# The attention branch's gate by 1024 columns, with block products on seven of sixteen k-tile pairs

## The chip, the cores and the metric

The kernel runs on one core of one Trainium2 chip. The metric is device time in microseconds (us), the median of several executions. Lower is better.

## The reference

One block of a hybrid transformer, in float32, for 256 tokens of width 2048 with a context of 256 tokens. The block normalises and modulates its input (an adaptive layer norm whose shift, scale and gate vectors come from `silu(c) @ w_ada`), projects it with `w_in`, runs a bidirectional gated recurrence (8 heads) and a windowed attention (8 heads) beside one another, merges the two branches, and ends in a convolutional feed-forward part. What matters here is the merge:

```
def gated_merge(y_rec, y_att, gate_rec, gate_att, w_rec, w_att, w_o):
    y = jax.nn.sigmoid(gate_rec) * (y_rec @ w_rec) + jax.nn.sigmoid(gate_att) * (y_att @ w_att)
    return y @ w_o
```

`gate_att` is a slice of the input projection: the modulated input (256 x 2048) times a 2048 x 2048 matrix. `y_rec @ w_rec` and `y_att @ w_att` contract over 1024.

## The kernel before

**Numbers as two halves.** TensorE multiplies rounded float32. Every operand is held as a high part (`hi`, a rounded copy) and a low part (`lo`, the rest), and `mm3` (L72) makes one product of three matmuls: high by high, high by low, low by high. A weight block arrives as 128 x 1024 float32 values in a buffer `raw` (five of them); ScalarE copies it to `whi` and VectorE subtracts to get `wlo` (three buffers each). Below, "a product" is such a three-matmul `mm3` on one 128 x 128 tile of activations and 512 columns of weights.

**The order of the work.** The program is written as one long Python trace. A scheduler orders the instructions of each engine at build time by priority (the place in the trace) and readiness; at run time every engine takes its list strictly in order. `tc.high_priority(offset=n)` moves instructions forward by n places; weight loads are moved by `LEAD` = 60, modulation steps by `LAG` = 60 the other way, a few evacuations by `RUSH` = 120. `issue_after` keeps an order on one engine.

**Weights.** `Stream.load` (L110) fetches the next 1024 columns of the weight stream on SP's queue and splits them. `chunk` (L141) does the same for parts that need something else in front of the split: it calls `make(raw)`, then casts and subtracts, each after the chunk before it (`behind`). Both read the same stream `wst`, whose order is laid down by the host code (L1207 to L1245).

**Modulation steps.** The vectors of the later modulations (gate 1, scale 2, shift 2, gate 2) are not made by TensorE matmuls but one block at a time: `ada_steps` (L387) is a generator with 8 groups of 19 steps. Sixteen steps of a group each load 512 KB of `w_ada` through POOL's DMA queue into a buffer `araw` and add it, times one column of `silu(c)`, to `acc` on VectorE (L405, L407). Two steps do nothing, and the last one transposes `acc` with TensorE and reduces it (L415 to L422). `ada(n)` takes n steps; it is called in many places, and `Stream.load` calls it too, once for every 16 points, where each load adds `st.pace` points. `homes[0]` says how many buffers the steps may use: 4 (two `araw` buffers and the tiles tagged `kT` and `va`) or 2 (the `araw` buffers alone). Groups 0 to 3 must be done when the merged result is added to x, groups 4 and 5 at its tile 10, the rest when the down projection begins.

**Small tasks.** Work such as transposing a result or the inner steps of a recurrent head is put in the list `tasks`; `tick` runs one at fixed points of the big matmul loops, for instance once per pass of `natural` (L466).

**The stages around the change.** The recurrent heads h = 0 to 7 (L691 to L722): for each, two loops `tform_all` of 48 matmuls, with `hgrn_a` (ScalarE and VectorE) behind each and `hgrn_b` to `hgrn_e` as tasks; after each `hgrn_a`, `ada(1)` for heads 0, 6 and 7 and `ada(2)` for heads 1 to 5 (L713), then `ada(1)` per head. Then attention, the recurrent output's gate, and the recurrent branch's merge gate (L820), four times 512 columns. Then the merge loop over four groups of 512 columns (L838 to L853): for each c, `columns()` makes the attention branch's gate (16 k-tiles, two blocks of 128 tokens, 96 matmuls) and applies a sigmoid; `columns(head(yre), 8)` makes the recurrent product (48 matmuls) and `columns(head(yat), 8)` the attention product (48); VectorE multiplies and adds (L845, L847, L848). All through this loop `st.pace` is 8, so every second load takes a modulation step. After it `xm` (x itself, 2 MB) is loaded into the tile tagged `qo`, which until then holds the recurrent output.

**The block product that exists already.** The first 32 of the 44 k-tiles of the feed-forward's down projection are done by `down_two` and `half` (L968, L1032). Two k-tiles and the two token blocks form a 2 x 2 block of activations, and two k-tiles and two groups of 512 columns a 2 x 2 block of weights. A normal pair takes 8 products. For the seven pairs in `SEVEN` a scheme with seven products is used: the activations are summed beforehand (`seven_acts`, L948), the weights on the fly by VectorE (`four`, L1010: four additions of 128 x 512, into two `araw` buffers), so three `chunk` splits beside the half one stand in place of two. Four banks `norm` and four banks `sev` collect the products, and eight VectorE additions and one copy (L1023 to L1030) join them.

**PSUM.** Eight banks: five in pool `mm` (`bankm`) and three in pool `ms` (`banks`).

Of the kernel before, what the change touches and what calls it, by code (L numbers as in the profile page):

```python
# [7 lines left out]
F32 = mybir.dt.float32  # L8
# [6 lines left out]
P = 128  # L15
# [20 lines left out]
SEVEN = (1, 3, 5, 7, 9, 11, 13)  # L36

# [14 lines left out]
def block_kernel(ctx, tc, xct, prm, cst, ada2, wst, out):  # L52
# [105 lines left out]
    def split(hi, lo, src):  # L158
        S.copy(hi, src)
        V.tensor_tensor(lo, src, hi.bitcast(F32), op=ALU.subtract)  # L160

# [529 lines left out]
    for h in range(H):  # L691
# [14 lines left out]
        for d in range(2):  # L706
            if 2 * h + d < 3:
                o = early_f[2 * h + d]
            else:
                o = bank()  # L710
                tform_all(o)
            hgrn_a(h, d, o)
            ada(1 if h > 5 or not h else 2)  # L713
# [104 lines left out]

    grn = gr.rearrange("p (c a b) t -> p c a (b t)", c=4, a=2)
    for c in range(4):  # L820
# [8 lines left out]
        if c == 2:  # L829
# [25 lines left out]
    st.pace = 0  # L855
    with tc.issue_after(sig.ins):
# [111 lines left out]
    def half(g0, g1, norm, sev, y, own):  # L968
# [4 lines left out]

        def add(b, a, w, start=False, stop=False):
            mm3(b, *a, *w, start, stop)
        first = SEVEN[0]
        for p in range(16):
            k1, k2 = 2 * p, 2 * p + 1
            rb, (w21, w22) = chunk(2, fetch)
            a11, a21, a12, a22 = act(k1, 0), act(k1, 1), act(k2, 0), act(k2, 1)  # L980
            if p not in SEVEN:
                st0, sp = p == 0, p == 15
                if sp:
                    ra, (w11, w12) = chunk(2, fetch)
                    for b, u1, u2, v1, v2 in ((0, a11, a12, w11, w21), (1, a11, a12, w12, w22), (2, a21, a22, w11, w21),
                                              (3, a21, a22, w12, w22)):
                        add(norm[b], u1, v1)
                        add(norm[b], u2, v2, stop=True)
                    break
                add(norm[0], a12, w21, st0)  # L990
                add(norm[2], a22, w21, st0)
                add(norm[1], a12, w22, st0)
                add(norm[3], a22, w22, st0)
                ra, (w11, w12) = chunk(2, fetch)
                add(norm[0], a11, w11)
                add(norm[2], a21, w11)
                add(norm[1], a11, w12)
                add(norm[3], a21, w12)
                continue
            f, l = p == first, p == SEVEN[-1]  # L1000
            d = sums[p]
            s1, s2, s4 = [(d[:, 0, i * P:i * P + P], d[:, 1, i * P:i * P + P]) for i in range(3)]
            add(norm[0], a12, w21)
            add(norm[1], s4, w22)
            ra, (w11,) = chunk(1, fetch, home=own)
            add(sev[0], a11, w11, f, l)

            r4 = strm.tile([P, 1024], F32, name="araw", bufs=2)

            def four(raw):  # L1010
# [249 lines left out]
```

## Time and profile before

| | |
|---|---|
| Median of 3 runs | 1665.86 us (1665.86 to 1666.29) |
| Profiled execution | 1666.65 us, of which its span is 1664.9 us |
| Granted TensorE clock | 1.00 |
| Matmuls | 8981, PE busy 99% of the span |
| VectorE (DVE) busy | 75% |
| ScalarE (ACT) busy | 50% |
| DMA | 372.83 MB, mean 224 GB/s |
| Merge loop, three of its four groups | 683.0 to 819.6 us |

PE stands for TensorE's matmuls and PEld for its weight loads, which run beside them. A group of instructions is named by line, engine, operation and `out<-in` with the program's tile names; behind the bar stand busy time, the mean duration of one in ns, and the time that the engine stood idle just before them, with what ended that wait. Rows of stretches (A:B) give busy time and, in brackets, instructions of each engine, then the granted clock, the DMA engines' share and GB/s. Matmuls are pipelined and overlap in the record, so their pitch is read from start times and not from durations. Nearly all matmuls come from the helper on L70, and all split copies and subtractions from L115, L116, L149 and L150; they are told apart by tile names.

### The profile page before, as it was taken

The numbers are of one execution on the slowest core, as the hardware profiler recorded it, in microseconds if no ns is written. First come the engines' busy times: TensorE is split into PE (matmuls) and PEld (weight loads), VectorE is DVE, ScalarE is ACT, GpSimd is POOL, SyncE is SP. The second block draws the span as 40 slices with busy tenths as digits, with TensorE's granted clock in tenths as the row PEclk, the third lists the DMA queues.
The fourth block names the chain that finished last, engine by engine and source line by source line (L and its number), as shares of the span: only waits on it lengthen the run. The fifth ranks groups of instructions, "written<-read, shape, count | busy, mean of one in ns | idle before, by whom it ended". The sixth has DMA issues, their size and how long they took to land.

```text
span 1664.9 us, 23855 instructions
## 1 busy us (share of the span) xinstructions
PE 1648.2 (99%) x8981; PEld 1369.6 (82%) x8981; DVE 1241.8 (75%) x1914; ACT 838.2 (50%) x1267; POOL 68.1 (4%) x132
## 2 busy tenths in 40 slices
PE   8999999999999999999999999999999999999998
PEld 4668888888888888888888988888888888888887
DVE  3448986666879876768769887788776888986655
ACT  4336543444645654444445665555555555545542
POOL 0000100000000000001100000000000000000000
PEclk9999999999999999999999999999999999999999
DMA  9996834534466666977856567577555665655554
GB/s 379 407 372 233 301 114 156 189 114 152 165 214 210 223 213 227 335 238 277 286 203 232 186 216 266 200 278 263 192 180 187 202 214 197 222 196 190 187 189 148
DMA packets 104723, 372.83 MB, mean 224 GB/s; under 512 B 11536, under 2 KB 13728, under 8 KB 104608
## 3 DMA queue, kind: packets, MB, share of 16 engines
q1 hardware_dynamic: 86176, 304.20, 51.8%
q0 software_dynamic: 18432, 67.12, 12.4%
q8 instruction: 70, 1.15, 0.3%
q14 instruction: 45, 0.37, 0.1%
HBM read 369.16 MB, written 2.11 MB: 223 GB/s over the span
## 4 chain that ended last, share of the span: by engine, by line
PE 89%; DVE 4%; issue 3%; DMA 2%; ACT 1%; POOL 0%; SPq 0%; DVEq 0%; ACTq 0%; POOLq 0%
PE bankm L70 78%; PE banks L70 9%; DVE wlo L116 1%; DMA ringv<-in_wst_dram 1%; DMA ringkT<-in_wst_dram 1%; DVE acc L407 1%; PE banks L782 0%; PE banks L415 0%; DMA araw<-in_ada_dram 0%; DMA ringq<-in_wst_dram 0%; PE banks L615 0%; PE banks L810 0%; PE banks L607 0%; DMA xraw<-in_xct_dram 0%; PE banks L1080 0%
## 5 line engine op out<-in xcount | busy, mean ns | idle before, releaser
L116 DVE TENSOR_TENSOR wlo<-raw,whi 128x1024 fp32r<-128x1024 f32 (+2 forms) x410 | 499.0, 1218 | 228.7 <-ACT whi L115 225.5
L115 ACT CAST whi<-raw 128x1024 fp32r<-128x1024 f32 (+2 forms) x410 | 428.3, 1045 | 459.0 <-PE bankm L70 411.7
L70 PE MATMUL bankm<-hl,whi 128*128 128x512 f32 (+1 forms) x2048 | 627.7, 389 | 0.1
L70 PE MATMUL bankm<-whi,hl 128*128 128x512 f32 x1640 | 526.4, 393 | 1.0 <-ACT hl L252 0.9
L70 PE MATMUL bankm<-hl,wlo 128*128 128x256 f32 (+2 forms) x1760 | 396.6, 293 | 1.5 <-DVE wlo L116 1.5
L70 PEld LDWEIGHTS bankm<-hl,wlo 128*128 128x128 f32 x1760 | 330.8, 188 | 75.6 <-DVE wlo L116 2.4
L70 PEld LDWEIGHTS bankm<-whi,hl 128*128 128x128 f32 x1640 | 307.4, 188 | 66.1 <-ACT hl L252 2.6
L70 PEld LDWEIGHTS bankm<-hl,whi 128*128 128x128 f32 x2048 | 327.8, 189 | 17.8 <-DVE fs L916 0.4
L70 PE MATMUL bankm<-wlo,hl 128*128 128x512 f32 x820 | 320.3, 391 | 0.0
L70 PEld LDWEIGHTS bankm<-wlo,hl 128*128 128x128 f32 x820 | 154.1, 188 | 31.2 <-DVE wlo L116 0.2
L407 DVE SCALAR_TENSOR_TENSOR acc<-araw,csil,acc 128x1024 f32<-128x1024 f32 x120 | 153.5, 1279 | 2.1 <-DMA araw<-in_ada_dram 1.7
L150 DVE TENSOR_TENSOR wlo<-raw,whi 128x1024 fp32r<-128x1024 f32 x74 | 90.2, 1224 | 41.2 <-ACT whi L149 38.9
L402 POOL DMA_DIRECT2D araw<-in_ada_dram x128 | 67.9, 531 | 1091.4 <-DVE acc L407 569.3
L149 ACT CAST whi<-raw 128x1024 fp32r<-128x1024 f32 x74 | 77.7, 1053 | 66.4 <-PE bankm L70 41.1
L70 PE MATMUL bankm<-yb,whi 128*128 128x512 f32 x256 | 80.9, 397 | 0.0
L70 PEld LDWEIGHTS bankm<-yb,wlo 128*128 128x128 f32 x256 | 48.1, 188 | 11.2
L929 ACT ACTIVATE fs<-fs,prm 128x256 f32<-128x256 f32 x44 | 26.4, 601 | 52.0 <-DVE fs L464 52.0
L70 PE MATMUL bankm<-yb,wlo 128*128 128x256 f32 x256 | 50.6, 279 | 0.0
L149 ACT CAST whi<-araw 128x1024 fp32r<-128x1024 f32 x28 | 29.4, 1052 | 39.0 <-DVE araw L1012 34.9
L70 PE MATMUL banks<-whi,hl 128*128 128x512 f32 x136 | 46.3, 389 | 0.0
L70 PE MATMUL bankm<-whi,g 128*128 128x512 f32 x124 | 41.3, 390 | 0.0
L70 PEld LDWEIGHTS bankm<-yb,whi 128*128 128x128 f32 x256 | 39.2, 189 | 0.1
(291 smaller groups left out, 1523.3 us busy)
## 6 DMA issues: line engine op xcount, KB each, us to landing
raw<-in_wst_dram SPq DMA_DIRECT2D x489, 512.0 KB, 4.1
araw<-in_ada_dram POOLq DMA_DIRECT2D x128, 512.0 KB, 4.7
ringv<-in_wst_dram SPq DMA_DIRECT2D x24, 512.0 KB, 10.0
ringq<-in_wst_dram SPq DMA_DIRECT2D x20, 512.0 KB, 9.9
araw<-in_wst_dram SPq DMA_DIRECT2D x10, 512.0 KB, 9.9
xraw<-in_xct_dram SPq DMA_DIRECT2D x8, 512.0 KB, 6.9
raw<-in_wst_dram SPq DMA_DIRECT2D x7, 384.0 KB, 9.9
ringkT<-in_wst_dram SPq DMA_DIRECT2D x5, 512.0 KB, 9.9
```

The lines of the kernel that those rows point to most:

```text
L70: return PE.matmul(o, l, r, start=start, stop=stop, skip_group_check=True)
L115: S.copy(hi, raw)
L116: self.last = V.tensor_tensor(lo, raw, hi.bitcast(F32), op=ALU.subtract)
L149: a = S.copy(hi[:, w], raw[:, w])
L150: b = V.tensor_tensor(lo[:, w], raw[:, w], hi[:, w].bitcast(F32), op=ALU.subtract)
L402: nc.gpsimd.dma_start(raw, ada2[idx])
L407: V.scalar_tensor_tensor(acc, raw, csil[:, kt, 0:1], acc, op0=ALU.mult, op1=ALU.add)
L929: S.activation(t, s, AF.Identity, bias=cb[:, f:f + 1], scale=cw[:, f, 1:2])
```

## The change

`half` is taken out of the end of the kernel and made general: it gets the function that picks activations, the number of pairs, the list of pairs done by seven products, their sums, the banks, the destination and the buffer for a lone half chunk. The down projection uses it as before. The merge loop now uses it for the attention branch's gate: for c = 0 and c = 2 it makes 1024 columns at once (8 pairs of k-tiles, two token blocks, four destination tiles `y`), with pairs 2, 4 and 6 by seven products for c = 0 and pairs 0, 2, 4 and 6 for c = 2. The sigmoids of all four tiles follow; c = 1 and c = 3 find theirs ready.

The sums of the activations are made once for both by four new tasks, `gate_sums`, which run in the last group of the recurrent branch's merge gate. They lie in a tile tagged `qo`, which `xm` takes afterwards. The half chunk's buffer takes the tag `kT`, so the modulation steps have two buffers (`homes[0] = 2`) through the merge loop.

Since `chunk` does not add to the pace, the 16 modulation steps that fell into the gates' columns are no longer taken there: `ada(2)` becomes `ada(3)` in heads 1 to 5, which is ten steps, and the other six fall to the calls behind the merge loop. The host lays the gate's weights out in the order in which the pairs read them.

```
+GSEVEN = (2, 4, 6), (0, 2, 4, 6)
...
+    def half(act, n, seven, sums, banks, y, own):
+        norm, sev = banks
...
+        for p in range(n):
+            k1, k2 = 2 * p, 2 * p + 1
+            rb, (w21, w22) = chunk(2, fetch)
+            a11, a21, a12, a22 = act(k1, 0), act(k1, 1), act(k2, 0), act(k2, 1)
+            st0 = p == 0
+            if p not in seven:
...
+            f, l = p == seven[0], p == seven[-1]
+            if f:
+                sev = sev()
+            s1, s2, s4, *s3 = sums[p]
+            add(norm[0], a12, w21, st0)
+            add(norm[1], s4, w22, st0)
+            ra, (w11,) = chunk(1, fetch, home=own)
+            add(sev[0], a11, w11, f, l)
+            r4 = strm.tile([P, 1024], F32, name="araw", bufs=2)
+            def four(raw):
+                V.tensor_tensor(raw[:, 0:512], ra[:, 0:512], ra[:, 512:], op=ALU.add)
+                V.tensor_tensor(raw[:, 512:], ra[:, 512:], rb[:, 512:], op=ALU.add)
+                V.tensor_tensor(r4[:, 0:512], raw[:, 0:512], rb[:, 512:], op=ALU.add)
+                V.tensor_tensor(r4[:, 512:], r4[:, 0:512], rb[:, 0:512], op=ALU.add)
+            r2, (t1, t3) = chunk(2, four, "araw")
+            add(sev[1], s1, t1, f, l)
+            add(sev[3], s3[0] if s3 else a21, t3, f, l)
+            _, (t2, t4) = chunk(2, lambda raw: None, r4)
+            add(sev[2], s2, t2, f, l)
+            add(norm[2], a22, t4, st0)
...
-            ada(1 if h > 5 or not h else 2)
+            ada(1 if h > 5 or not h else 3)
...
+    def gate_sums(p):
+        if not gsums:
+            gsums["all"] = big.tile([P, 4, 2, 4 * P], F32R, name="sx", tag="qo")
+        d = gsums["all"][:, len(gsums) - 1]
+        x = scr.tile([P, 512], F32, name="t")
+        w = scr.tile([P, 512], F32, name="t")
+        V.tensor_tensor(x.rearrange("p (k t) -> p k t", k=2), hl[:, 2 * p:2 * p + 2, 1, :].bitcast(F32),
+                        hl[:, 2 * p:2 * p + 2, 0, :].bitcast(F32), op=ALU.add)
+        a11, a21, a12, a22 = [x[:, i * P:i * P + P] for i in range(4)]
+        V.tensor_tensor(w[:, 0:P], a21, a22, op=ALU.subtract)
+        V.tensor_tensor(w[:, P:2 * P], a11, w[:, 0:P], op=ALU.subtract)
+        V.tensor_tensor(w[:, 2 * P:3 * P], a12, w[:, P:2 * P], op=ALU.subtract)
+        V.tensor_tensor(w[:, 3 * P:], a21, a11, op=ALU.subtract)
+        split(d[:, 0, :], d[:, 1, :], w)
+        gsums[p] = parts_of(d[:, 0], d[:, 1])
...
+            tasks += [lambda p=p: gate_sums(p) for p in (2, 4, 6, 0)]
...
+    homes[0] = 2
+    gown = big.tile([P, 2, 512], F32R, name="gone", tag="kT")
+    gown = [gown[:, i] for i in range(2)]
     for c in range(4):
-        gas = []
-        for o in columns():
-            ga = scr.tile([P, 512], F32, name="t")
-            sig = S.activation(ga, o, AF.Sigmoid)
-            gas.append(ga)
+        if c % 2 == 0:
+            norm = [bank() for _ in range(4)]
+            y = [scr.tile([P, 512], F32, name="t") for _ in range(3)] + [scr.tile([P, 512], F32, name="rs", bufs=1)]
+            half(tok, 8, GSEVEN[c // 2], gsums, (norm, lambda: [bank()] + [bank(ms) for _ in range(3)]), y, gown)
+            for o in y:
+                sig = S.activation(o, o, AF.Sigmoid)
         for tt, o in enumerate(columns(head(yre), 8)):
             V.tensor_tensor(grn[:, c, tt, :], grn[:, c, tt, :], o, op=ALU.mult)
         for tt, o in enumerate(columns(head(yat), 8)):
-            V.tensor_tensor(gas[tt], gas[tt], o, op=ALU.mult)
-            V.tensor_tensor(grn[:, c, tt, :], grn[:, c, tt, :], gas[tt], op=ALU.add)
+            ga = y[2 * tt + c % 2]
+            V.tensor_tensor(ga, ga, o, op=ALU.mult)
+            V.tensor_tensor(grn[:, c, tt, :], grn[:, c, tt, :], ga, op=ALU.add)
...
+    homes[0] = 4
     with tc.issue_after(sig.ins):
         S.preload_act_table_set("natural_log_exp_and_others")
...
+    gat = ga_a.reshape(8, 2, P, 2, 1024)[:, ::-1].transpose(3, 0, 1, 2, 4).reshape(2, 16, P, 1024)
     for c in range(4):
-        parts += [gat[c], wr[c], wt[c]]
+        parts += ([gat[c // 2]] if c % 2 == 0 else []) + [wr[c], wt[c]]
```

More of the change, by code (lines that the diff above doesn't have):

```diff
@@ L162, in exp_silu, with parts_of @@
+    def parts_of(hi, lo):
+        return [(hi[:, i:i + P], lo[:, i:i + P]) for i in range(0, hi.shape[-1], P)]
     def exp_silu(dst, src, tmp):
@@ L817, in turned @@
             V.scalar_tensor_tensor(lo, o2, scale, hi.bitcast(F32), op0=ALU.mult, op1=ALU.subtract)
+    gsums = {}
+    def gate_sums(p):
[13 more added lines that the diff above has]
+        gsums[p] = parts_of(d[:, 0], d[:, 1])
     grn = gr.rearrange("p (c a b) t -> p c a (b t)", c=4, a=2)
@@ L966, in up, with down_two @@
             up_evac(g, gt, i, *duo((h2, h2)))
-    def half(g0, g1, norm, sev, y, own):
+    def down_two(g0, g1):
+        own = big.tile([P, 2, 512], F32R, name="wone", tag="acc")
+        own = [own[:, i] for i in range(2)]
         def act(k, tt):
@@ L972, in act @@
             return gt[:, k % 16, 1, ts], gt[:, k % 16, 0, ts]
[L974 to L1010, printed above, removed]
-                V.tensor_tensor(raw[:, 0:512], ra[:, 0:512], ra[:, 512:], op=ALU.add)
-                V.tensor_tensor(raw[:, 512:], ra[:, 512:], rb[:, 512:], op=ALU.add)
-                V.tensor_tensor(r4[:, 0:512], raw[:, 0:512], rb[:, 512:], op=ALU.add)
-                V.tensor_tensor(r4[:, 512:], r4[:, 0:512], rb[:, 0:512], op=ALU.add)
-            r2, (t1, t3) = chunk(2, four, "araw")
-            add(sev[1], s1, t1, f, l)
-            add(sev[3], a21, t3, f, l)
-            _, (t2, t4) = chunk(2, lambda raw: None, r4)
-            add(sev[2], s2, t2, f, l)
-            add(norm[2], a22, t4)
-            if l:
-                S.copy(y[0], sev[0])
-                V.tensor_tensor(y[2], sev[2], y[0], op=ALU.subtract)
-                V.tensor_tensor(y[1], sev[1], y[2], op=ALU.add)
-                V.tensor_tensor(y[2], sev[3], y[2], op=ALU.add)
-                V.tensor_tensor(y[3], sev[3], y[1], op=ALU.add)
@@ L1028, in half @@
-        with tc.high_priority(offset=RUSH):
-            for b in range(4):
-                V.tensor_tensor(y[b], norm[b], y[b], op=ALU.subtract if b == 2 else ALU.add)
-    def down_two(g0, g1):
-        own = big.tile([P, 2, 512], F32R, name="wone", tag="acc")
-        own = [own[:, i] for i in range(2)]
+        both = {p: parts_of(sums[p][:, 0], sums[p][:, 1]) for p in SEVEN}
         sev = [bank()]
@@ L1038, in down_two @@
         y0 = [scr.tile([P, 512], F32, name="t") for _ in range(3)] + [scr.tile([P, 512], F32, name="rs", bufs=1)]
-        half(g0, g1, norm, sev, y0, own)
+        half(act, 16, SEVEN, both, (norm, lambda: sev), y0, own)
         norm = [bank()] + [bank(ms) for _ in range(3)]
@@ L1043, in down_two @@
         y1 = [y1[b // 2][:, b % 2] for b in range(4)]
-        half(g0, g1, norm, sev, y1, own)
+        half(act, 16, SEVEN, both, (norm, lambda: sev), y1, own)
         return y0, y1
@@ L1228 @@
     parts += [aqh[0], aqh[1], flat(_nat(np, gg)), flat(_nat(np, ga_r))]
-    gat, wr, wt = _nat(np, ga_a), _nat(np, g["w_rec_proj"][0]), _nat(np, g["w_att_proj"][0])
+    wr, wt = _nat(np, g["w_rec_proj"][0]), _nat(np, g["w_att_proj"][0])
+    gat = ga_a.reshape(8, 2, P, 2, 1024)[:, ::-1].transpose(3, 0, 1, 2, 4).reshape(2, 16, P, 1024)
     for c in range(4):
-        parts += [gat[c], wr[c], wt[c]]
+        parts += ([gat[c // 2]] if c % 2 == 0 else []) + [wr[c], wt[c]]
     parts.append(_duos(np, _tiles_t(np, g["w_out"][0])))
```

28 lines of the change are left out of this document (added).

## The prediction

> **What bounds the kernel now.** I read the page first (span, busy shares, the chain that ended last, the costliest groups).
>
> ```profile
> span 1664.9 us, 23855 instructions
> PE 1648.2 (99%) x8981; PEld 1369.6 (82%) x8981; DVE 1241.8 (75%) x1914; ACT 838.2 (50%) x1267; POOL 68.1 (4%) x132
> PEclk9999999999999999999999999999999999999999
> PE 89%; DVE 4%; issue 3%; DMA 2%; ACT 1%; POOL 0%; SPq 0%; DVEq 0%; ACTq 0%; POOLq 0%
> ...
> L70 PE MATMUL bankm<-whi,hl 128*128 128x512 f32 x1640 | 526.4, 393 | 1.0 <-ACT hl L252 0.9
> ```
>
> The matmul queue sets the end: 89% of the chain is PE, its clock is granted in full in every slice, and the form that makes the gate (weights `whi` moving, activations `hl` stationary) stood idle 1.0 us in 1640 matmuls. So a matmul taken out is worth its pitch, wherever the queue stays fed. Since busy matmuls overlap, I take the pitch from start times, in the two down-projection halves that already use the block product (timeline, then busy time by stretch: one normal and one seven-product pair each).
>
> ```profile
> 1313.10 0.84 PE L70 MATMUL bankm<-wone,hl 128*128 128x512 f32 x3
> 1313.78 0.39 PE L70 MATMUL banks<-whi,sb 128*128 128x512 f32 x1
> ```
>
> ```profile
> core 0: us, PE busy (x) PEld busy (x) DVE busy (x) ACT busy (x) POOL busy (x), PEclk, DMA share, GB/s
> 1294.95:1305.85 10.90, 10.65 (x47) 7.84 (x45) 9.21 (x13) 7.13 (x11) 0.00 (x0) 1.00 0.58 194
> 1305.85:1316.04 10.19, 10.19 (x46) 8.44 (x45) 9.78 (x13) 5.67 (x8) 0.00 (x0) 1.00 0.62 208
> 1316.04:1326.22 10.18, 10.18 (x46) 8.45 (x45) 9.14 (x10) 5.77 (x7) 0.00 (x0) 1.00 0.63 206
> ```
>
> Three matmuls take 13.78 - 13.10 = 0.68 us, 0.227 each. A normal pair is 24 of them, a seven-product pair 21: 45 x 0.2267 = 10.2 us, which is what a steady stretch takes (edges add one to the count). VectorE is busy 9.14 of 10.18 there and still in time. Only the first stretch, where the block product begins, took 0.72 us longer.
>
> **The change part by part.** *Removed matmuls.* Each of the four 512-column gates was 96 matmuls. Now two gates of 1024 columns take 5 normal and 3 seven-product pairs, then 4 and 4: 183 + 180 = 363 against 384. **21 x 0.2267 = 4.76 us off the path.** The weight bytes and transposes stay the same in number.
>
> The Trainium skill ("TensorE: Matmul & The Clock Gate", Back-to-back issue gap) puts a sustained stream of weight loads and matmuls at about 131 ns a matmul for 512 columns, and calls 216 ns the isolated gap. By 131 ns the saving would be an estimated 2.75 us instead. The timeline above, 227 ns in such a stream, disagrees, and decides.
>
> *VectorE in the two new halves.* Its work per stretch is known from the same stage:
>
> ```profile
> L150 DVE TENSOR_TENSOR wlo<-raw,whi 128x1024 fp32r<-128x1024 f32 x16 | 19.6, 1224 | 3.8 <-ACT whi L149 2.9
> L150 DVE TENSOR_TENSOR wlo<-araw,whi 128x1024 fp32r<-128x1024 f32 x10 | 12.2, 1222 | 0.3
> L150 DVE TENSOR_TENSOR wone<-raw,wone 128x512 fp32r<-128x512 f32 x5 | 3.4, 685 | 0.0
> L1011 DVE TENSOR_TENSOR araw<-raw 128x512 f32<-128x512 f32 x5 | 3.4, 684 | 0.0
> ```
>
> A normal pair is two 1224 ns subtractions; the end of a half adds eight 128x512 operations at 0.685, 5.5 us. First half: 3 x 9.14 + 2 x 2.45 + 5.5 = 37.8 us in 183 x 0.2267 = 41.5. Second: 4 x 9.14 + 5.5 = 42.1 in 40.8. The excess 1.3 us is that end work, which feeds no matmul of the half; it only frees banks, and the ScalarE copy of `sev[0]` frees one first, the early subtraction of `norm[0]` (finished 18 matmuls, 4.1 us, before the half ends) the next. I cost the end at 0, as that cover is longer than an operation; without it, up to 1.4 us each.
>
> *Entering a half.* The first begins with two normal pairs: 10.9 us in which VectorE owes 4.9, so it can catch up by 6.0. The work before it grows by the sums: four times two 128x512 operations and four 128x128 ones.
>
> ```profile
> 639.00:661.00 22.00, 22.00 (x110) 18.11 (x109) 16.84 (x21) 10.14 (x12) 2.12 (x4) 1.00 0.70 241
> 661.00:683.00 22.00, 22.00 (x98) 18.21 (x97) 14.73 (x13) 9.75 (x11) 2.11 (x4) 1.00 1.02 392
> 683.00:728.50 45.50, 45.50 (x206) 37.66 (x205) 34.32 (x33) 19.28 (x21) 4.22 (x8) 1.00 0.82 283
> 728.50:774.00 45.50, 45.50 (x210) 37.63 (x209) 31.37 (x33) 18.89 (x20) 2.64 (x5) 1.00 0.71 244
> ```
>
> ```profile
> L934 DVE TENSOR_TENSOR fs<-fs,fs 128x256 f32<-128x256 f32 x44 | 18.6, 424 | 2.7
> L418 DVE TENSOR_TENSOR modv<-modv,prm 128x8 f32<-128x8 f32 x1 | 0.2, 162 | 0.0
> L407 DVE SCALAR_TENSOR_TENSOR acc<-araw,csil,acc 128x1024 f32<-128x1024 f32 x120 | 153.5, 1279 | 2.1 <-DMA araw<-in_ada_dram 1.7
> ```
>
> A 128x128 operation lies between 0.16 and 0.42; I take the middle, 0.29, so one set is 2 x 0.685 + 4 x 0.29 = 2.5 us and four are 10.1. The last recurrent gate (661 to 683) had 14.73 busy, so 24.8 of 22: 2.8 us over, less than the 6.0 that the two normal pairs give. Price 0, as long as no other 3.2 us comes with it. The lone half chunk's buffer takes `kT`, so it also waits for the last modulation step there; pair 2 comes 10.9 us into the half, and the same 6.0 us cover that step's 1.28.
>
> The second half starts with a seven-product pair at once. Before it, gates 0 and 1 without their own columns hold (34.32 + 31.37) - 16 x 1.224 - 8 x 1.28 = 35.9 us of VectorE in 91.0 - 43.5 = 47.5: not full. Its first block product waits for a PSUM bank that the last attention product of gate 1 still holds: three operations of 0.685 after one 1.22 subtraction at worst, 3.3 us, less the six matmuls (1.4) that go first, 1.9. So entry costs between 0 (a steady stretch) and 0.72 + 1.9 = 2.6; I take **0.72**, the one entry the trace shows.
>
> *Modulation steps.* Blocks fetched by `chunk` do not count for the pace, so 16 steps leave the gate stage: 10 go to heads 1 to 5, 6 further back (up-projection tiles 23 to 27).
>
> ```profile
> araw<-in_ada_dram POOLq DMA_DIRECT2D x128, 512.0 KB, 4.7
> ```
>
> Each step issues one 512 KB DMA on POOL's queue, 4.7 us to landing, and one 1.28 us operation. Heads 1 to 5 get 12.8 us of VectorE and 5.2 MB:
>
> ```profile
> 208.00:241.00 33.00, 32.71 (x284) 27.12 (x283) 26.96 (x71) 17.84 (x37) 1.06 (x2) 1.00 0.27 89
> 241.00:274.00 33.00, 33.00 (x228) 27.91 (x227) 27.69 (x59) 13.01 (x27) 2.64 (x5) 1.00 0.56 189
> 274.00:322.00 48.00, 48.00 (x219) 39.99 (x218) 26.40 (x31) 15.79 (x27) 4.75 (x9) 1.00 0.58 196
> 322.00:366.00 44.00, 44.00 (x336) 36.51 (x335) 33.68 (x83) 21.98 (x43) 1.06 (x2) 1.00 0.26 87
> 433.00:455.00 22.00, 21.47 (x130) 17.74 (x129) 20.68 (x42) 14.50 (x31) 2.64 (x5) 1.00 0.67 227
> ```
>
> From 208 to 366 it was idle 158 - 114.7 = 43.3 us: price 0, and without that cover 12.8 at most. The six that go back leave the sixth group complete only at tile 8 of the merged sum, the last call before its use at tile 10; two tiles of matmuls cover it, else a landing and an operation, 4.7 + 1.28. The tight place is head 7 (433 to 455): PE lost 0.53 to VectorE there.
>
> ```profile
> 454.20 0.33 PE L607 MATMUL banks<-cst,hb 128*128 128x128 f32 x1 [0.53 <-DVE hb L572]
> ```
>
> The shift by 10 puts there steps 55 to 60 of 19-step groups: two empty ones, the transposes and the first of a group in place of six multiply-adds, so less VectorE work. I count 0, with a gain of up to 0.53.
>
> *Queues.* The sums take the buffer that `xm` (two 1 MB loads on SP's queue) needs, so these leave after the second half instead of at 651 us.
>
> ```profile
> L860 SPq DMA_DIRECT2D xm<-in_xct_dram x2: 384/495/606, 651.4 to 654.4; - x2
> 669.06 1.05 ACT L115 CAST whi<-raw 128x1024 fp32r<-128x1024 f32 x1 [2.93 <-DMA raw<-in_wst_dram]
> ```
>
> Weight fetches queue behind them, and ScalarE waited 2.93 us for one; PE was busy all through 661 to 683 all the same, covered by the split tiles ahead. Without that cover it is 2.9 at most. I take 0; `xm` itself has gates 2 and 3, over 40 us.
>
> *Sum.* -4.76 + 0.72 = **-4.04 us**: span 1660.86. The profiled run took 1666.65, so 1.75 lies around its span: 1662.61. The timed median stands 0.79 below that run: **1661.8 us**.
>
> **The rivals.** (B) *The saving in full or more*: entry costs nothing and head 7's 0.53 goes: 1665.86 - 5.29 = 1660.6. For it: 13 VectorE operations stood in the stretch that began late, left over from the up-projection, and these are not here. Against: the second half is entered without a normal pair.
>
> (C) *Given back in small waits*: both entries cost 0.72 and the second also its 1.9 of bank wait: 1665.86 - 4.76 + 3.34 = 1664.4. For it: VectorE is fuller in the second half than in the steady stretches. Against: 34 us of steady alternation without a stall.
>
> (D) *Slower: the two `araw` buffers.* The block product needs both for its summed weights, and modulation steps, no longer allowed the other two homes, use the same two. If steps left over from gate 1 hold them, the second half's first sums wait for a landing and an operation, 4.7 + 1.28 = 6.0 us each; two steps are 12.0. Behind them in the lists of ScalarE and VectorE stand all later splits, since `chunk` keeps their order, and TensorE waits for those. It decides once the delay passes the lead of two split tiles, 24 matmuls or 5.4 us: then 1665.86 - 4.04 + 12.0 - 5.4 = 1668.4. For it: POOL waits on these buffers most of its time.
>
> ```profile
> POOL araw L402 <- DVE acc L407: 569.3, 100, 56.7
> ```
>
> Against: VectorE has over 10 us free in gates 0 and 1 to finish them.
>
> (E) *A removed matmul gives less than its pitch*, because weight loads pace the queue. Then each is worth its busy share in the page, 1369.6/8981 = 0.152 us, 3.2 for the 21, and less the entry 2.5: 1663.4. Against: 45 matmuls in 10.18. The Trainium skill, in the section named above, has the spacing set by weight load and matmul together, which is this case's rule.
>
> **How the numbers follow.** Forecast 45% (own range 1661.1 to 1662.5), B 12%, C 29%, D 12%, E 2%. About 0.2%, 3.3 us, is what a measurement of this kernel can tell from no change. Faster by more is the forecast and B, 57%; within it C and E, 31%; slower D, 12%. Low end: B's 1660.6, less 0.2 for the timing spread of 0.43: 1660.4. High end: through C up to about half of D, 1667.0; this leaves out some 6% above and as much below.
>
> **What would show it.** The profile after should have 8960 matmuls; a steady stretch of 10.2 us in both gate halves; gates 0 to 3 about 4 us shorter from the first sigmoid's stage to the first `xm` operation; PE busy without idle in heads 1 to 5. C shows as gaps where the second half begins, with a wait on a bank or on a `whi` or `wlo`; D as VectorE or ScalarE idle in front of the sums, released by `araw` or its DMA; B as none of these. The forecast is wrong if the stage gains its 4 us and the total does not (then the moved steps cost it in heads 1 to 7), or if PE stands more than 1.4 us in the halves.

## The result and the profile after

The changed kernel takes 1672.02 us (median of 6 runs, 1669.66 to 1672.26), the kernel before in the same series 1665.86 (6 runs, 1664.77 to 1666.29). The ratio is 1.0033, 95% interval 1.0022 to 1.0043: **slower by 6.2 us**, where 4 us less were forecast, and above the range. The profiled execution of the changed kernel is the fastest of its six (1669.66 us), so its trace need not show the whole of the 6.2 us.

From the page of the changed kernel: span, busy time of each engine, and the group of the modulation steps. All later line numbers are this kernel's: products L71, splits L116, L117, L150 and L151, the four weight sums L204 to L207, a step's operation L473.

```profile
span 1667.9 us, 23899 instructions
PE 1648.4 (99%) x8960; PEld 1366.4 (82%) x8960; DVE 1284.4 (77%) x1996; ACT 852.8 (51%) x1287; POOL 68.4 (4%) x132
...
L473 DVE SCALAR_TENSOR_TENSOR acc<-araw,csil,acc 128x1024 f32<-128x1024 f32 x120 | 153.2, 1277 | 1.8 <-DMA araw<-in_ada_dram 1.5
```

The 21 matmuls are gone (8960), the steps are the same 120 with the same duration, and yet the span is 3.0 us longer. TensorE's waits (sum in us, times, longest) have new entries:

```profile
PE banks L71 <- ACT whi L150: 3.8, 2, 3.6
...
PE banks L71 <- DVE hb L635: 0.7, 2, 0.5
PE banks L71 <- DVE hb L621: 0.6, 2, 0.4
...
PE bankm L71 <- ACT whi L116: 0.2, 1, 0.2
```

For comparison, the rows of the same view of the kernel before, whose lines are L70, L116 and L555:

```profile
PE bankm L70 <- DVE wlo L116: 1.5, 2, 0.8
...
PE banks L70 <- DVE hb L555: 0.3, 1, 0.3
```

The wait for `whi` of 3.6 us is new. The ones for `hb`, which belong to the recurrent heads, have grown, and two of them are in new places. The 1.5 us of the kernel before are two waits in the first projections (151 and 161 us), ahead of all that was changed; some of the profiles used here have them and some do not: the kernel before's has them, the changed kernel's has not.

Where the 3.0 us arose can be read from two marks: the last sigmoid of the recurrent branch's gate, and the first operation on `xm` behind the merge loop. Each row gives the first and the last start; the kernel before first, the changed kernel second.

```profile
L828 ACT ACTIVATE gr<-bankm x4: 584/594/600, 636.3 to 663.3; 128x512 f32<-128x512 f32 x4
...
L872 DVE SCALAR_TENSOR_TENSOR xm<-bankm,modv,xm x32: 473/477/485, 852.2 to 932.4; 128x256 f32<-128x256 f32 x32
```

```profile
L912 ACT ACTIVATE gr<-bankm x4: 583/592/600, 638.8 to 665.3; 128x512 f32<-128x512 f32 x4
...
L963 DVE SCALAR_TENSOR_TENSOR xm<-bankm,modv,xm x32: 473/476/486, 855.3 to 935.4; 128x256 f32<-128x256 f32 x32
```

| part of the span | before | after | difference |
|---|---|---|---|
| up to the first mark | 663.3 | 665.3 | +2.0 (+3.5 without the two early waits) |
| between the marks: the changed stage | 188.9 | 190.0 | +1.1 |
| behind the second mark | 812.7 | 812.6 | -0.1 |

The marks are operations of ScalarE and VectorE, and the first comes 0.5 us later behind TensorE's own work in the changed kernel. TensorE's matmuls, counted in the trace, are sharper. The merge loop, from its first matmul to the first one on `yb`, has 768 of them before (662.16 to 840.13 us, 177.97) and 747 after (663.62 to 843.16, 179.54): 1.6 us more. At 170 us, when the two early waits lie behind, the changed kernel is 1.6 us ahead of the kernel before at the same matmul; at the loop's first one it is 1.5 us behind, so 3.1 us are lost between.

So two things went wrong, and apart from one another. The heads, in which nothing was changed but where ten steps stand, lost about 3.1 us. And the stage that has 4.76 us less to do took 1.6 us more, so it lost 6.3 somewhere.

**The place in the stage.** TensorE's timeline where the second half begins (start, duration, operation; in brackets the idle time before it and what ended it):

```profile
754.19 0.40 PE L71 MATMUL banks<-whi,sx 128*128 128x512 f32 x1
758.16 0.80 PE L71 MATMUL banks<-whi,sx 128*128 128x512 f32 x1 [3.57 <-ACT whi L150]
```

It waited 3.57 us for the cast of `t2, t4`, the second pair of weight sums. VectorE's timeline says why these were late:

```profile
745.08 0.68 DVE L482 TENSOR_REDUCE modv<-banks 128x4 f32<-128x512 f32 x1
...
746.46 1.28 DVE L473 SCALAR_TENSOR_TENSOR acc<-araw,csil,acc 128x1024 f32<-128x1024 f32 x1
...
750.00 0.68 DVE L205 TENSOR_TENSOR araw<-raw 128x512 f32<-128x512 f32 x1
...
753.62 0.68 DVE L938 TENSOR_TENSOR gr<-gr,rs 128x512 f32<-128x512 f32 x1
754.22 1.28 DVE L473 SCALAR_TENSOR_TENSOR acc<-araw,csil,acc 128x1024 f32<-128x1024 f32 x1
755.53 0.69 DVE L206 TENSOR_TENSOR araw<-araw,raw 128x512 f32<-128x512 f32 x1
756.26 0.69 DVE L207 TENSOR_TENSOR araw<-araw,raw 128x512 f32<-128x512 f32 x1
```

One group of steps ends here (L482) and the next begins, with the first step (L471) at 745.67 and the second at 746.46. Of the four sums, L204 and L205 run at 749.39 and 750.00; before L206 come five operations for the attention product and the first pair, and then another **step**. POOL's queue shows the load of that step's block:

```profile
746.72 0.53 POOL L468 DMA_DIRECT2D araw<-in_ada_dram  x1 [33.31 <-DVE modv L484]
```

The first two blocks of the new group had lain in the two `araw` buffers since their loads were issued at 710.55 and 712.88, because their steps had to stand behind the old group's transposes and reductions. As soon as the first was read, the third block was loaded into its buffer (the row names L484, which ends 0.1 us behind L471), and it landed 3.8 us later, at 750.5. The program has only these two buffers. L204 and L205 write one of them and L206 still reads it, so L206 and L207 write the other, the one with the step's block, and could not run before the step had read it.

So the second pair of sums is ready at 757, when TensorE has used up all that it had at 754.6. What stands in between is nothing that VectorE waited for: it is busy without a gap. Busy time by stretch (PE, PEld, VectorE, ScalarE, POOL, granted clock, DMA share, GB/s):

```profile
744.50:755.00 10.50, 10.09 (x45) 7.91 (x43) 10.50 (x16) 2.62 (x3) 0.53 (x1) 1.00 0.48 150
755.00:758.20 3.20, 0.04 (x1) 0.04 (x1) 1.95 (x4) 1.14 (x2) 0.00 (x0) 0.99 0.11 19
758.10:761.60 3.50, 3.40 (x7) 2.30 (x8) 3.46 (x3) 1.97 (x4) 0.00 (x0) 0.51 0.45 149
761.60:772.00 10.40, 10.40 (x47) 8.59 (x47) 8.38 (x11) 5.89 (x7) 0.00 (x0) 1.00 0.59 203
```

The third row is the second part of the loss: right behind the stall the granted clock is 0.51, for 3.4 us, and 7 matmuls are started where 15 would be. The page's forty slices do not show it, since each is 42 us long.

### The profile page after: what moved, and what is told of

Read it like the earlier page. It is cut to its first block, busy times and chain, and to the rows that moved or that the text cites. A ratio compares the mean times of both kernels' runs of the same rounds, so it can differ in the third digit from the quotient of the medians.

```text
span 1667.9 us, 23899 instructions
## 1 busy us (share of the span) xinstructions
PE 1648.4 (99%) x8960; PEld 1366.4 (82%) x8960; DVE 1284.4 (77%) x1996; ACT 852.8 (51%) x1287; POOL 68.4 (4%) x132
## 4 chain that ended last, share of the span: by engine, by line
PE 92%; DVE 4%; DMA 2%; issue 1%; ACT 1%; SPq 0%; ACTq 0%; DVEq 0%
PE bankm L71 78%; PE banks L71 11%; DMA ringv<-in_wst_dram 1%; DVE wlo L117 1%; DVE acc L473 1%; DMA ringq<-in_wst_dram 1%; PE banks L848 0%; PE banks L681 0%; PE banks L481 0%; PE banks L673 0%; ACT whi L116 0%; DMA xraw<-in_xct_dram 0%; PE banks L876 0%; PE banks L1112 0%; PE banks L682 0%
## 5 line engine op out<-in xcount | busy, mean ns | idle before, releaser
L71 PE MATMUL bankm<-hl,whi 128*128 128x512 f32 (+1 forms) x2048 | 627.6, 389 | 0.1
L117 DVE TENSOR_TENSOR wlo<-raw,whi 128x1024 fp32r<-128x1024 f32 (+1 forms) x378 | 459.1, 1216 | 184.2 <-ACT whi L116 180.7
L116 ACT CAST whi<-raw 128x1024 fp32r<-128x1024 f32 (+1 forms) x378 | 394.4, 1045 | 397.5 <-PE bankm L71 347.4
L71 PE MATMUL bankm<-whi,hl 128*128 128x512 f32 x1556 | 501.1, 393 | 1.2 <-ACT hl L318 1.0
L71 PE MATMUL bankm<-hl,wlo 128*128 128x256 f32 (+2 forms) x1760 | 396.1, 293 | 0.0
L71 PEld LDWEIGHTS bankm<-hl,wlo 128*128 128x128 f32 x1760 | 330.6, 188 | 73.9 <-DVE wlo L117 0.5
L71 PEld LDWEIGHTS bankm<-whi,hl 128*128 128x128 f32 x1556 | 291.7, 188 | 63.9 <-ACT hl L318 2.6
L71 PEld LDWEIGHTS bankm<-hl,whi 128*128 128x128 f32 x2048 | 327.6, 189 | 17.5 <-DVE fs L1007 0.4
L71 PE MATMUL bankm<-wlo,hl 128*128 128x512 f32 x778 | 303.4, 391 | 0.0
L71 PEld LDWEIGHTS bankm<-wlo,hl 128*128 128x128 f32 x778 | 146.4, 188 | 29.3 <-DVE wlo L117 0.2
L151 DVE TENSOR_TENSOR wlo<-raw,whi 128x1024 fp32r<-128x1024 f32 x99 | 120.7, 1223 | 49.6 <-ACT whi L150 46.3
L473 DVE SCALAR_TENSOR_TENSOR acc<-araw,csil,acc 128x1024 f32<-128x1024 f32 x120 | 153.2, 1277 | 1.8 <-DMA araw<-in_ada_dram 1.5
L150 ACT CAST whi<-raw 128x1024 fp32r<-128x1024 f32 x99 | 104.1, 1054 | 83.3 <-PE bankm L71 51.5
L71 PE MATMUL bankm<-yb,whi 128*128 128x512 f32 x256 | 80.8, 397 | 0.0
L150 ACT CAST whi<-araw 128x1024 fp32r<-128x1024 f32 x42 | 44.1, 1053 | 65.3 <-DVE araw L205 54.3
L71 PEld LDWEIGHTS bankm<-yb,wlo 128*128 128x128 f32 x256 | 48.1, 188 | 11.3
L151 DVE TENSOR_TENSOR wlo<-araw,whi 128x1024 fp32r<-128x1024 f32 x42 | 51.2, 1221 | 2.9 <-ACT whi L150 1.7
L71 PE MATMUL bankm<-yb,wlo 128*128 128x256 f32 x256 | 50.6, 279 | 0.0
L71 PE MATMUL banks<-whi,hl 128*128 128x512 f32 x136 | 46.3, 389 | 0.0
L71 PE MATMUL bankm<-whi,g 128*128 128x512 f32 x124 | 41.3, 389 | 0.0
```

The lines of the kernel that those rows point to most:

```text
L71: return PE.matmul(o, l, r, start=start, stop=stop, skip_group_check=True)
L116: S.copy(hi, raw)
L117: self.last = V.tensor_tensor(lo, raw, hi.bitcast(F32), op=ALU.subtract)
L150: a = S.copy(hi[:, w], raw[:, w])
L151: b = V.tensor_tensor(lo[:, w], raw[:, w], hi[:, w].bitcast(F32), op=ALU.subtract)
L473: V.scalar_tensor_tensor(acc, raw, csil[:, kt, 0:1], acc, op0=ALU.mult, op1=ALU.add)
```

## The experiments

All times are medians, with the ratio to the kernel before on the same chip and its 95% interval. The kernel before took 1666.21 us beside the first four, 1666.04 beside the next three, 1665.58 beside the three after these and 1666.79 beside the last two. Unless another base is named, an edit is made to the changed kernel.

**Steps out of the two buffers.** In the merge loop the steps take the tile tagged `va` in place of the two `araw` buffers.

```
+                    elif homes[0] == 1:
+                        raw = big.tile([P, 1024], F32, name="araw", tag="va")
...
-    homes[0] = 2
+    homes[0] = 1
```

> The changed kernel, with the modulation steps of the merge loop loaded into the free tile tagged va in place of the two araw buffers; all other work and its amount as in the changed kernel (1672.0 us; its profiled span 1667.9). Buffer theory: the second half's first sums wait because a modulation step holds one of the two araw buffers; TensorE then stands 3.6 us and its clock is halved for 3.4 us more, 5.8 us in all. Then the stall and the half clock go, span about 1662.1, time 1663 to 1664.5. Load theory: VectorE simply has too much to do where the second half begins; its work is the same here, so a stall of 3 us or more stays there and the time is 1670 to 1672. Theory of the moved steps: the ten steps in heads 1 to 5 cost the time; nothing changes, 1670 to 1672.

Measured: 1672.08 us, 1.0036 (1.0024 to 1.0049). The place at 754 us is clean, no step stands between the sums, and the time is the same all the same: with one buffer the steps' loads come late, and VectorE, which takes its list in order, waits for them. Its waits, in the first row, and two of TensorE's (of the four for `wlo`, two are the early ones at 151 and 161 us; the others are at 722 and 813):

```profile
DVE acc L475 <- DMA araw<-in_ada_dram: 18.6, 9, 4.2
```

```profile
PE bankm L71 <- DVE wlo L117: 2.8, 4, 0.8
PE banks L878 <- DVE gr L940: 1.4, 2, 0.8
```

The edit thus took one cause away and put another in. It supports rival D's claim on the buffers: the group of steps still ends at the entry (its last reduction starts at 747.78) and VectorE is still full behind it (10.00 of 10.00 us from 755 to 765), yet TensorE does not stall there. It does not test the claim alone, since the steps behind that end also come later.

**A normal pair first.** The second half uses pairs 2, 4 and 6 as the first does, so it has three more matmuls and two normal pairs ahead of its first block product.

```
-GSEVEN = (2, 4, 6), (0, 2, 4, 6)
+GSEVEN = (2, 4, 6), (2, 4, 6)
```

> The changed kernel with pairs 2, 4 and 6 by seven products in both halves, so that the second half too begins with two normal pairs (three matmuls more, +0.7 us). Buffer theory: the steps left over are finished in those 10.9 us and the buffers are free when the first sums come; no stall, 1664 to 1665.5. Load theory: the same, VectorE catches up in the two normal pairs. Theory of the moved steps: 1671 to 1673.

Measured: 1666.26 us, 1.0001 (0.9992 to 1.0009). The same place, by stretch:

```profile
744.50:755.00 10.50, 10.50 (x50) 8.69 (x49) 9.56 (x13) 4.40 (x6) 0.53 (x1) 1.00 0.65 205
755.00:765.20 10.20, 10.20 (x46) 8.45 (x46) 9.10 (x11) 4.67 (x5) 0.00 (x0) 1.00 0.52 174
```

No stall, the clock in full. Between the two marks it needs 184.9 us (667.4 to 852.3), 4.0 less than before for 18 matmuls fewer. TensorE's own count of the loop gives 174.51 against 177.97 us, 3.5 less. Against the changed kernel's 190.0 the marks give 5.1 less, and with the 3 x 0.227 that it does more, **the entry of the second half cost 5.8 us**. Yet the total is only that of before: what this stage gains is lost ahead of it, where TensorE again falls 3.1 us behind between 170 us and the loop, and the moved steps are what both kernels have there.

**No steps in gate 1.** The pace is 0 in the second group of the merge loop and doubled in the fourth.

```
     for c in range(4):
+        st.pace = (8, 0, 8, 16)[c]
```

> The changed kernel with no modulation step taken during gate group 1 and twice as many in group 3, so that none is left over where the second half begins; the number of steps in the merge loop stays 16. Buffer theory: no stall and no half clock there, 1663 to 1664.5, unless the eight steps of group 3 run into the merged sum. Load theory: the same or a smaller stall, 1663 to 1667. Theory of the moved steps: 1670 to 1672.

Measured: 1670.86 us, 1.0024 (1.0015 to 1.0034). Again the entry is clean, and again the loss turns up where the steps went: about 6 us between 820 and 860, among others

```profile
PE bankm L71 <- DVE yb L161: 2.2, 1, 2.2
PE bankm L71 <- DVE wlo L117: 1.5, 2, 1.1
```

**The moved steps alone.** The kernel before, with nothing of the block product.

```
-            ada(1 if h > 5 or not h else 2)
+            ada(1 if h > 5 or not h else 3)
```

> The kernel before with three modulation steps in place of two behind each hgrn_a of heads 1 to 5, and nothing else changed. Buffer theory and load theory: the ten steps find VectorE idle and cost at most 1 us: 1665.0 to 1667.0. Theory of the moved steps: 1668 to 1672, with TensorE idle in the heads, released by VectorE.

Measured: 1669.66 us, 1.0022 (1.0013 to 1.0032): **3.45 us slower by this alone**, where the prediction has 0. Its profiled execution is the fastest of its ten (1667.77 us). Head 3 shows how. VectorE's timeline in this kernel:

```profile
255.03 1.27 DVE L407 SCALAR_TENSOR_TENSOR acc<-araw,csil,acc 128x1024 f32<-128x1024 f32 x1
256.22 0.68 DVE L543 TENSOR_TENSOR_SCAN hb<-cst,hb 128x256 f32<-128x256 f32 x1
...
258.59 1.28 DVE L407 SCALAR_TENSOR_TENSOR acc<-araw,csil,acc 128x1024 f32<-128x1024 f32 x1
259.79 0.42 DVE L555 TENSOR_TENSOR hb<-hb,qo 128x256 f32<-128x256 f32 x1
```

Two steps stand inside the head's chain, one ahead of its scan and one behind it. In the kernel before the scan follows L538 with no step between. TensorE's timeline there, first of this kernel, then of the kernel before:

```profile
260.99 0.71 PE L70 MATMUL banks<-hb 128*32 128x64 f32 x48
262.16 0.63 PE L70 MATMUL banks<-hb 128*32 128x64 f32 x16 [0.46 <-DVE hb L569]
```

```profile
263.15 0.94 PE L70 MATMUL banks<-hb 128*32 128x64 f32 x64
```

The head's 64 small matmuls ran as one burst and are now cut in two. TensorE's list has them at a fixed place among the big ones, so it cannot do those first. Head 4 has the same with 0.26 us at 333. And VectorE's idle time was not filled evenly. By stretch, two rows of those that the prediction quotes of before (26.40 and 33.68 busy there):

```profile
274.00:322.00 48.00, 48.00 (x224) 40.05 (x223) 19.76 (x27) 17.09 (x28) 1.58 (x3) 1.00 0.36 121
322.00:366.00 44.00, 43.74 (x329) 36.33 (x328) 43.39 (x92) 20.74 (x42) 6.33 (x12) 1.00 0.64 209
```

From 274 to 322, where long products run, it does less than before; in heads 4 and 5 it is busy 43.39 of 44.00 us. A third part is TensorE's own: one group's eight transposes (L415) now fall into head 6's burst.

```profile
430.14 0.71 PE L415 MATMUL banks<-cst,acc 128*128 128x128 f32 x5
430.78 0.46 PE L70 MATMUL banks<-hb 128*32 128x64 f32 x24
...
433.31 0.71 PE L70 MATMUL bankm<-hl,whi 128*128 128x512 f32 x2
```

From 430.14 to 433.31 are 3.17 us; the kernel before does its burst there in one piece, from 430.97 to 432.46, 1.49 us. Five transposes in a row start within 0.64 us, so eight are about 1.0, and 0.7 is lost by the alternation. With the two waits that makes 0.46 + 0.26 + 0.7, 1.4 of the 3.45. Beside the kernel before, matmul by matmul, TensorE falls 0.9 us behind in head 3 (263 to 271 us), 0.7 in head 4 (333 to 339) and 0.9 by the moved transposes (head 6's burst less their old place at 508), and 3.1 in all between 170 us and the merge loop; the remaining 0.6 were not traced one by one. The changed kernel, taken the same way, loses the same amounts at the same places.

**Steps between the heads.** If steps harm inside the heads' chains, the long value projections ahead of heads 4 and 6, which were taken to be free of heads' chains, should take them for nothing. Fifteen steps by the pace of their loads, 14 points for the first and 16 for the second; the heads keep `ada(2)`. First without the block product, on the kernel before:

```
             bs = [bank() for _ in range(4)]
+            st.pace, st.due = 14, 0
             natural(bs, range(4))
+            st.pace, st.due = 0, 0
```

> The kernel before with the same fifteen steps between the heads and nothing else changed. Theory (steps are free between the heads): 1665.5 to 1666.7. Rival (any earlier step costs in the heads): 1668 to 1670, as with ten steps behind hgrn_a.

Measured: 1669.3 us, 1.0019 (1.001 to 1.0027), 3.3 us slower. Head 7 now waits 1.5 us where it waited 0.5, and head 3 still has a step ahead of its scan, at 256.91.

```profile
PE banks L607 <- DVE hb L572: 1.5, 1, 1.5
```

What falls is the premise on the place. The first projection's 192 matmuls run from 251.8 to 300.8 us, and head 3's burst (from 262.9) stands among them; head 5's (from 361.2) stands in the second. A head's inner steps are tasks of the loop that follows it, so the first half of each projection is a head's chain too, and this run does not show what steps cost where no chain runs.

The same spread with the block products, once with a normal pair first and once with the change's own pairs and pace 0 in group 1 (`st.pace = (8, 0, 8, 8)[c]`):

> late_seven (seven products for pairs 2, 4 and 6 in both halves, 18 matmuls fewer than before), with ada(2) kept in heads 1 to 5 as in the kernel before, and fifteen steps taken instead by the loads of the two value projections between heads (seven before head 4, eight before head 6). Theory: the ten steps cost about 3.4 us because they stand in the lists next to the recurrent heads' short VectorE chains; between the heads VectorE is idle 40% of the time, so there they cost nothing. Then 18 x 0.227 = 4.1 us come out: 1661.8 to 1663. Rival: any earlier step costs the same wherever it stands, as the list of the heads shifts anyway; then 1665.5 to 1666.5 as late_seven.

> The changed kernel's own seven-product pairs (21 matmuls fewer), with the same fifteen steps between the heads, ada(2) in the heads, and no modulation step in gate group 1. Theory: neither the heads nor the second half's entry costs anything: 4.8 us come out, 1661.1 to 1662.5. Load theory of the entry (VectorE has too much to do there with or without a step): a stall of 1 us or more and perhaps a half clock at the second half, 1663 to 1667.

Measured: 1666.78 us, 1.0004 (0.9995 to 1.0013), and 1665.82 us, 0.9999 (0.999 to 1.0008). Both are where the kernel before is: the gain of the block product and the loss of the spread steps cancel.

**All sixteen steps behind the heads.** The heads keep `ada(2)`. The steps go to the recurrent branch's gate (its loads at pace 12 in two groups) and to the tiles of the merged sum, up to tile 13 (the split of `sh2` moves from tile 10 to 12 with them).

```
+        st.pace = 12 if c < 2 else 8
...
-        if 2 <= j < 10:
+        if j < 14:
             ada(2)
```

> late_seven (18 matmuls fewer than before; 1666.3 us) with no step moved to an earlier place: ada(2) in heads 1 to 5 as before; instead the recurrent branch's merge gate takes pace 12 in its first two groups (four steps more), and the merged sum takes two steps at tiles 0 to 12, where gates and sums wait for them. Until the merge gate every engine's list is that of the kernel before. Theory of the changed lists (a step more in front of the heads' chains, in lists whose order was fixed by modelled times, costs 3 us or more): that cost is gone, 18 x 0.227 = 4.1 us come out, 1661.8 to 1663. Rival (the block product itself costs what it saves, through VectorE, somewhere in the merge loop): 1665 to 1667.

The same with the change's own pairs, pace 0 in group 1 and `ada(3)` from tile 6; and that without either change of pace, so that the steps in gate 1 stay:

> The changed kernel's own pairs (21 matmuls fewer), ada(2) in heads 1 to 5, no step in gate group 1, pace 12 in the first two groups of the recurrent branch's merge gate and two or three steps at tiles 0 to 12 of the merged sum. Theory: neither the heads nor the second half's entry costs anything, 4.8 us come out, 1661.1 to 1662.3. Load theory of the entry: a stall of 1 us or more where the second half begins, 1662.5 to 1666. Rival (the merged sum cannot take the steps): TensorE idle between 842 and 930 us of the span, 1664 or more.

> As the one before, but with the steps of gate group 1 left in (pace 8 throughout), so that the number of steps in front of the second half is that of the changed kernel, in another phase: no group of steps ends there, so its reductions do not delay the last step past the first sums, and the list has the sums' four additions in one piece. Theory (the stall comes from one step that stands between the sums, not from the number of steps): no stall and no half clock, 1661.1 to 1662.5. Load theory (VectorE's amount of work there decides): the stall stays, 2 to 6 us, 1663.5 to 1667.

Measured: 1666.59 us, 1.0004 (0.9996 to 1.0013); 1666.82, 1.0005 (0.9996 to 1.0014); 1666.1, 1.0005 (0.9996 to 1.0014). Heads and entries are clean in all three. The third is telling: gate 1 has its steps at pace 8 as in the changed kernel, but a group does not end there, no step stands between the four sums, and TensorE does not stall:

```profile
747.62 0.68 DVE L206 TENSOR_TENSOR araw<-araw,raw 128x512 f32<-128x512 f32 x1
...
748.82 0.68 DVE L207 TENSOR_TENSOR araw<-araw,raw 128x512 f32<-128x512 f32 x1
```

```profile
744.50:755.00 10.50, 10.50 (x47) 8.51 (x46) 10.32 (x13) 5.88 (x8) 0.00 (x0) 1.00 0.48 160
```

L204 starts at 746.42, and between L206 and L207 stands one short operation. VectorE is as full here as in the changed kernel (10.32 us against 10.50), and from 715 to 745 it does more (25.39 us against 19.90). So neither the number of steps in gate 1 nor VectorE's amount of work made the stall, but **one step's place between the sums**.

The gain is lost at a new place: with steps up to tile 13 the sixth group of steps ends in the last tiles of the merged sum, and the sum of squares behind it is late. The row of TensorE's timeline is the first kernel's, that of busy time by stretch the second's:

```profile
928.92 0.70 PE L998 MATMUL banks<-rs,cst 128*128 128x256 f32 x2 [2.71 <-DVE rs L971]
```

```profile
930.00:940.00 10.00, 9.87 (x67) 9.27 (x68) 9.38 (x19) 6.60 (x16) 0.00 (x0) 0.83 0.18 55
```

All three stall there for 2.7 us. In the second and third the granted clock then falls to half, for 3.4 and 6.8 us, in the first it does not.

**The steps where nothing short waits.** The same idea without the late tiles: pace 12 in three groups of the recurrent branch's gate, and `ada(2)` or `ada(3)` in tiles 0 to 9 alone. First the change's own pairs, then a normal pair first.

```
-            ada(1 if h > 5 or not h else 3)
+            ada(1 if h > 5 or not h else 2)
...
+        st.pace = 12 if c < 3 else 8
...
-        if 2 <= j < 10:
-            ada(2)
+        if j < 10:
+            ada(3 if j in (2, 4) else 2)
```

> The changed kernel's own pairs (21 matmuls fewer), ada(2) in heads 1 to 5 as before, pace 12 in the first three groups of the recurrent branch's merge gate (six steps more) and twelve steps at tiles 0 to 8 of the merged sum in place of eight (none after tile 8, so that nothing stands before the last sum of squares). Every list up to the merge gate is that of the kernel before, and the list of the second half's entry has the four additions in one piece. Theory (the block product is worth its matmuls wherever no step stands in a chain that TensorE waits for): 4.8 us less the 0.8 seen at the two entries come out, 1661.5 to 1662.8. Rival (any place for the steps costs what the block product saves): 1665 to 1667, and the trace shows a new idle stretch of TensorE.

> The same with pairs 2, 4 and 6 in both halves (18 matmuls fewer). Theory: 0.7 us above the run before, 1662.2 to 1663.5. Rival: 1665 to 1667.

Measured: **1663.57 us**, 0.9986 (0.9977 to 0.9995), and **1662.98 us**, 0.9983 (0.9974 to 0.9992): 3.2 and 3.8 us faster than the kernel before beside them, 8.5 and 9 below the changed kernel's median, which was taken in another series. The two are not told apart; the second waits 1.1 us for a `wlo` at 831 us, which the first does not. From the page of the first (span 1660.8 us), the busy times, then one of TensorE's waits (the early ones) and the entry by stretch:

```profile
PE 1644.1 (99%) x8960; PEld 1365.2 (82%) x8960; DVE 1285.0 (77%) x1996; ACT 852.4 (51%) x1287; POOL 68.3 (4%) x132
```

```profile
PE bankm L71 <- DVE wlo L117: 1.1, 2, 0.8
```

```profile
738.00:748.50 10.50, 10.50 (x48) 8.70 (x47) 7.33 (x10) 4.12 (x5) 0.00 (x0) 1.00 0.47 146
748.50:758.70 10.20, 10.20 (x46) 8.27 (x45) 10.17 (x14) 5.20 (x6) 0.00 (x0) 1.00 0.60 196
```

VectorE does as much as in the changed kernel (1285.0 against 1284.4 us) and is just as full behind the entry, 10.17 of 10.20. TensorE loses nothing by it: L204 to L207 run from 745.66 to 748.74 with no step among them. Between the two marks this kernel takes 184.8 us against 188.9 before, and by TensorE's own count the loop takes 174.20 against 177.97, 3.8 less:

```profile
L913 ACT ACTIVATE gr<-bankm x4: 583/591/601, 636.7 to 663.3; 128x512 f32<-128x512 f32 x4
...
L964 DVE SCALAR_TENSOR_TENSOR xm<-bankm,modv,xm x32: 468/476/485, 848.1 to 928.2; 128x256 f32<-128x256 f32 x32
```

## Why the prediction was wrong

**Removed matmuls: right.** 8960 are left, and in the loop they start 227 ns apart in the median, before and after. Where the entry is clean, the stage gains 4.0 us for 18 and 4.1 for 21 by the marks, 3.5 and 3.8 by TensorE's own count; most of what is missing from the full pitch is at the ends of the halves (below). The Trainium skill's 131 ns a matmul ("TensorE: Matmul & The Clock Gate", Back-to-back issue gap), by which 18 would be worth an estimated 2.4 us, does not hold here: 3.5 / 18 is 194 ns and 4.0 / 18 is 222 ns.

**"Entering a half": wrong for the second half.** The sentence "entry costs between 0 (a steady stretch) and 0.72 + 1.9 = 2.6; I take 0.72" failed: it cost 5.8. The working added up VectorE's work in gates 0 and 1 (35.9 of 47.5 us) and found it "not full". Over 91 us that is so; in the 10.5 us that matter VectorE was busy 10.50, since a group of steps ended there, and a step stood between the sums. TensorE's starts give it directly. From 754.19 to 758.16 are 3.97 us where the pitch is 0.227, so the stall cost 3.7; the next seven starts take 3.48 us, up to 761.64, in place of 1.6, so the half clock behind it cost 1.9, a price that the sum had nowhere. Together they are 5.6, close to the 5.8 by the marks. Rival D named the place and the cause in kind, a step among the sums of the second half; its price was that of two late loads, and there was none: the step's load, issued at 746.72, landed 3.8 us later, ahead of the step by as much. What cost was the shared buffer together with VectorE's fixed order: the buffer put the step ahead of L206, and the list put five other operations ahead of the step, though its block was there. Whether the scheduler could have placed the step earlier, no run here shows.

**The first half's entry, the queues, the six steps that go back: right; the ends of the halves: nearly.** TensorE's only wait between the marks beside the 3.57 us is the 0.2 us for `whi` (L116), at 701 us; none is for a bank, `xm` or a weight load, and behind the second mark the two kernels differ by 0.1 us. At the ends of the halves, priced at 0, a few starts come late (699.7 to 701.4 and 792.0 to 793.7 us) and cost 0.5 and 0.2 us. One reading in the working of the first entry was off: the stretch from 661 to 683 that it calls the last recurrent gate is already the loop's first gate. The sums run in the stretch before, 639 to 661, with 16.84 us busy: 26.9 of 22, so 4.9 over instead of 2.8, still less than the 6.0 of cover.

**"Price 0" for the ten moved steps: wrong, 3.45 us** (3.1 in the traces of three kernels that have them). The argument was that VectorE was idle for 43.3 us from 208 to 366. That sum says nothing of where it is idle. Half of it, 21.6 us, lay from 274 to 322, where the steps did not go, and in heads 4 and 5 they filled VectorE up to 43.39 of 44.00. A 1.28 us step inside a head's chain of short operations, each waiting for the one before, delays all behind it; TensorE reaches the head's matmuls at the same place of its list and stands there. The bound "without that cover 12.8" held the truth between, but a value at its very end was chosen. Of head 7 the prediction expected at best a gain of 0.53: that wait is gone, and one of 0.42 us for L621 came 3 us later, at 457.3. The prediction had said what would show this ("then the moved steps cost it in heads 1 to 7").

**The sum.** On TensorE the stage has -4.76 for the matmuls, +5.6 for the entry and +0.7 for the ends of the halves, together +1.5, where +1.6 was measured. With 3.1 for the moved steps that makes +4.7; the spans differ by 3.0, since the kernel before's trace has the early waits, worth 1.6, and the changed kernel's has not. The medians differ by 6.2. The 1.5 left are not in the profiled execution, which is the fastest of the six, and stay open; early waits in the other five could be a part of them, but no run shows it.

**What remains of the forecast.** With the steps put elsewhere the change's own pairs give 3.2 us less than the kernel before beside them (interval 0.8 to 3.8) and a normal pair first gives 3.8 less (1.3 to 4.3), where the forecast has 4.0 and rival C 1.5. The stage's gain of 3.8 by TensorE's count is of the size forecast, but partly by luck: the first of these two kernels loses at most 0.1 us at either entry, where the sum put 0.72, and 0.7 at the ends of the halves, where it put 0.

## What to carry to other kernels

Idle time summed over a stage is no cover for an operation that goes into a fixed list: look at what it will stand in front of, and whether a chain that feeds the bounding engine runs there. When work moves, price the place where it goes by moving it alone. Here filler cost nothing measurable beside long products that are fed ahead (the recurrent branch's gate and the first tiles of the merged sum); it did harm inside short chains, between the parts of one operand, and right ahead of a deadline. A buffer that filler shares with the bounding work holds that work up for as long as the filler waits for its own turn.

## What the runs showed of the hardware

The long stall of TensorE was paid twice here. After 3.57 us without a matmul the granted clock was 0.51 from 758.1 to 761.6 us, and 1.9 us more were lost. The Trainium skill ("TensorE: Matmul & The Clock Gate", Part 1: The HAM clock gate) tells of a clock at half rate after an idle window of about 3.4 us, taken from a free-running window of 3413 ns; the length of the slow stretch agrees with it. But stalls of 2.7 us, shorter than such a window, were also followed by the half clock in two of three profiled executions, for 3.4 and 6.8 us; what decided there, no run here shows.
